# Layer 1's SwiGLU FFN: gate and up by seven block products instead of eight, with the second products set between the next chunk's first ones

## The chip, the cores and the metric

One core of a Trainium2 chip runs the program. The metric is the device time of one execution in microseconds; the kernel before took 1693.99 us in the median of three runs (1692.38 to 1694.93). Matrix products run on TensorE, the rest on VectorE, ScalarE and GpSimd; DMAs are issued from SyncE's queue (SP).

## What is computed

A two-layer backbone over 512 latent tokens and 256 context tokens of width 1024. Each layer mixes tokens in four head groups and then applies a modulated SwiGLU FFN with 2816 hidden columns, 22 tiles of 128. The change is in the FFN of the latent tokens in the second layer (layer 1), the last work before the output:

```python
def swiglu(h, w_in_, w_out_):
    gate, up = jnp.split(h @ w_in_, 2, axis=-1)
    return (jax.nn.silu(gate) * up) @ w_out_
...
    x = x + g_a * rms_norm(mix_x @ w_out, norm_g[1])
    x = x + g_f * rms_norm(swiglu(modulate(rms_norm(x, norm_g[2]), sh_f, sc_f), w_ffn_in, w_ffn_out), norm_g[3])
```

All of it is float32.

## The kernel before

**Numbers as hi and lo.** Matrices are kept as a rounded hi and the rest lo (`split`, L363: hi on ScalarE, L366; lo on VectorE or GpSimd, L367). A product of 128 rows is three matmuls (`mac3`): hi by hi (L425), hi by lo (L426 or L427) and lo by hi. In them the weights of a hidden tile are the stationary operand and the tokens the moving one, 512 columns, or 256 where a product is made in halves of the tokens.

**Weights.** `weights` (L372) loads a raw unit (512 KB for eight 128 by 128 tiles) into one of four buffers of the pool `wr` and splits it in two pieces of 512 columns into the pools `wh` (five buffers) and `wl` (four). `lo_pool` alternates the engine of the lo. `prefetch` loads units early into slots of their own (`wt`).

**The FFN** (`ffn`, L1462; called from `layer_end`). The 22 hidden tiles come in chunks, `fcx`: (0, 8), (8, 15), (15, 22). For each hidden tile j there are two units, gate and up, each a product over eight k tiles: 48 matmuls into two PSUM tiles. `ffn_gate` (L1452) makes tanh on ScalarE (L1456), two VectorE instructions on PSUM and SBUF (L1457, L1458) and a split into `g` (L369, L370). In layer 1 the first three tiles (`first1`) are made in halves of the tokens, since the second half of the activations `hf` is ready later. After a chunk's hidden tiles come its eight second products (one for each 128 columns of the output), 3 matmuls for each hidden tile of the chunk, added into `y` by `evac_y` (L1404 on ScalarE for the first chunk, L1406 on VectorE for the others). The last chunk's last five are made in halves again, then `ends` applies the norm and the residual (L545, L546) and stores x. The stream x stays in SBUF all the time.

**Order.** A scheduler of the framework sets the order of each engine's instructions from the dependences and the order of the program; buffers of pools are given out in turn, so a load waits until the last reader of the buffer's former content is done.

Of the kernel before, what the change touches and what calls it, by code (L numbers as in the profile page):

```python
# [21 lines left out]
P = 128  # L22
D = 1024
KT = D // P
# [11 lines left out]
# how the work is cut and which engine takes what  # L36
# [24 lines left out]
 'preu1': 4,  # L61
# [46 lines left out]
 'por': '1023'}  # L108
# [20 lines left out]
class Half:  # L129
    """Half a slot; the slot is given back with the second of them."""  # L130
# [10 lines left out]
class Arena:  # L141
    """Equal slots of SBUF, taken and given back in program order."""
# [35 lines left out]
class HL:  # L178
    """A float32 matrix [K, N] as hi + lo, in tiles of 128 rows."""
# [21 lines left out]
class F32T:  # L201
    """A float32 matrix [K, N] in tiles of 128 rows."""
# [15 lines left out]

class Stream:
# [3 lines left out]
class Build:  # L223
    def __init__(self, tc, es, I, out, dbg=None):
# [7 lines left out]
        self.wl = pool("wl", bufs=T["wl"])  # L232
        self.ap = pool("arena", bufs=1)
# [23 lines left out]
    def scale(self, c, out, in_, col):  # L257
        """out = in_ * col on the engine that c names."""
# [75 lines left out]
    def load_params(self, l, p=None):  # L334
        """The layer's small parameters; those of the norms first."""
# [26 lines left out]
    def split(self, hi, lo, src, scale=None, eng=None):  # L362
        """hi = round(src * scale), lo = src * scale - hi; both exact in float32r."""  # L363
# [8 lines left out]
    def weights(self, src, shape, hold=False):  # L372
        """A unit of weights from DRAM: shape[0] matrices of shape[1] columns as (hi, lo). With hold in slots, until freed."""
# [29 lines left out]
    def prefetch(self, units, hold=0):  # L403
        """Loads the units that the next calls of weights ask for, the first ones held in slots."""
# [5 lines left out]
    def tick(self):  # L410
        """Emits work of the background at its rate."""
# [11 lines left out]
    def mac3(self, out, lh, ll, rh, rl, first, last):  # L423
        nc = self.nc
        nc.tensor.matmul(out, lh, rh, start=first, stop=False)  # L425
        nc.tensor.matmul(out, lh, rl, start=False, stop=False)  # L426
        nc.tensor.matmul(out, ll, rh, start=False, stop=last)  # L427

    def dense(self, out, w, a, t0, n, w0=0, nk=KT, late=False, ks=None):
        """out[128, n] = w^T a over nk tiles of rows, tokens t0..t0+n; w from its tile w0 on. With late a's lo comes last."""  # L430
        nc = self.nc
        ks = ks or range(nk)
        for i in ks:
            f, z = i == ks[0], i == ks[-1]
            ah, al = a.h[i][:, t0:t0 + n], a.l[i][:, t0:t0 + n]
# [15 lines left out]
    def rsqrt(self, y, v, tag):  # L451
        """y = 1/sqrt(v) on small tiles of float32."""
# [3 lines left out]
    def rms(self, tiles, t0, n):  # L456
        """PSUM tile [128, n]: rstd of the tokens t0..t0+n in every partition; tiles: 8 of [128, .]."""
# [5 lines left out]
    def square(self, sq, k, x, n, t0=0, full=None, evac=False):  # L463
        """Squares of x, tile k of 8, for columns t0..t0+n: two sums, of the even and of the odd tiles, but for the last two."""
# [23 lines left out]
    def rms_end(self, parts, n, norm=False):  # L488
        """The same from the squares, in parts to be summed."""
# [28 lines left out]
    def modnorm(self, st, h, A, B, t0, n):  # L518
        """h (hi, lo) = rms_norm(x) * A + B for the tokens t0..t0+n of the stream."""
# [15 lines left out]
    def residual(self, st, y, G, t0, n, sq):  # L535
        """x += G * rms_norm(y) for the tokens t0..t0+n."""
# [1324 lines left out]
```

## Time and profile before

| | |
|---|---|
| runs (3) | 1694.93, 1693.99, 1692.38 us; median 1693.99 |
| span of the profiled execution | 1692.6 us (the page has no other time of it) |
| TensorE busy | 1624.3 us, 96%, 9935 matmuls |
| VectorE, ScalarE, GpSimd busy | 944.4, 740.5, 607.2 us |
| read from and written to HBM | 209.14 MB, 4.19 MB |

A busy share is an average over stages; what a stage is limited by is read from the stretch itself, and there from who waits for whom. Recorded matmuls overlap: what one costs is seen from one start to the next. The stretch of the change begins near 1337 us and goes to the end.

### The profile page before, as it was taken

How to read it: one execution, taken by the hardware profiler on the slowest of the kernel's cores; microseconds unless marked ns; L12 is line 12 of the kernel's file. 1: busy time of each engine (PE TensorE's matmuls, PEld its weight loads, DVE VectorE, ACT ScalarE, POOL GpSimd, SP SyncE). 2: the span in 40 equal slices, each digit the busy share in tenths (PEclk: the TensorE clock that was granted, in tenths of full speed). 3: DMA queues.
4: the chain of work that ended last, by engine and by line, in shares of the span. 5: the costliest groups of instructions: out<-in, count | busy, mean ns of one | idle time of the engine just before them, and what ended most of it. 6: DMA issues, size and time to landing. Idle time of an engine off the chain costs nothing.

```text
span 1692.6 us, 27131 instructions
## 1 busy us (share of the span) xinstructions
PE 1624.3 (96%) x9935; PEld 1381.3 (82%) x9935; DVE 944.4 (56%) x2172; ACT 740.5 (44%) x1658; POOL 607.2 (36%) x691
## 2 busy tenths in 40 slices
PE   6899999999999999999999998999798999999997
PEld 2876778787989998888888888999578988888887
DVE  4876675858685569542443466758765531232344
ACT  3654456654445655333332334465565433332331
POOL 2421333664466565322222225332425322222233
PEclk9999999999999998999999998999799999999998
DMA  9554564254466423334334452122042122323221
GB/s 315 178 181 154 190 222 125 98 176 129 148 230 184 148 74 116 112 138 149 138 127 150 137 201 95 59 73 70 2 132 81 38 93 94 98 82 107 92 95 51
DMA packets 81045, 215.10 MB, mean 127 GB/s; under 512 B 10512, under 2 KB 18576, under 8 KB 80912
## 3 DMA queue, kind: packets, MB, share of 16 engines
q1 hardware_dynamic: 80912, 213.37, 38.3%
q8 instruction: 78, 1.28, 0.3%
q14 instruction: 55, 0.45, 0.1%
HBM read 209.14 MB, written 4.19 MB: 126 GB/s over the span
## 4 chain that ended last, share of the span: by engine, by line
PE 83%; DVE 8%; DMA 3%; issue 2%; ACT 2%; POOL 1%; SPq 0%; DVEq 0%; POOLq 0%; ACTq 0%
PE mm L425 22%; PE mm L427 22%; PE mm L426 22%; PE ms L584 2%; PE mx L1097 2%; PE mm L437 1%; PE mx L1091 1%; PE mm L438 1%; DMA wm_m<-in_wmod_dram 1%; PE mx L1349 1%; PE mm L449 1%; PE mm L443 1%; PE mm L442 1%; PE mm L444 1%; DVE wl L367 1%
## 5 line engine op out<-in xcount | busy, mean ns | idle before, releaser
L366 ACT ACTIVATE wh<-wr 128x512 fp32r<-128x512 f32 (+3 forms) x526 | 318.9, 616 | 581.5 <-PE mm L426 478.9
L367 POOL TENSOR_TENSOR wl<-wr,wh 128x512 fp32r<-128x512 f32 (+2 forms) x248 | 322.8, 1304 | 666.1 <-PE mm L427 517.8
L367 DVE TENSOR_TENSOR wl<-wr,wh 128x512 fp32r<-128x512 f32 (+3 forms) x278 | 206.7, 747 | 180.5 <-PE mm L427 131.5
L425 PE MATMUL mm<-hfh_m,wh 128*128 128x512 f32 (+1 forms) x656 | 253.7, 387 | 0.0
L426 PE MATMUL mm<-hfl_m,wh 128*128 128x512 f32 (+1 forms) x656 | 253.5, 386 | 0.0
L427 PE MATMUL mm<-hfh_m,wl 128*128 128x512 f32 (+1 forms) x656 | 253.4, 386 | 0.0
L425 PEld LDWEIGHTS mm<-hfh_m,wh 128*128 128x128 f32 x656 | 123.7, 188 | 26.5
L427 PEld LDWEIGHTS mm<-hfh_m,wl 128*128 128x128 f32 x656 | 123.5, 188 | 26.5
L426 PEld LDWEIGHTS mm<-hfl_m,wh 128*128 128x128 f32 x656 | 123.5, 188 | 26.5
L425 PE MATMUL mm<-gh_m,wh 128*128 128x512 f32 x275 | 108.3, 394 | 0.0
L426 PE MATMUL mm<-gl_m,wh 128*128 128x512 f32 x275 | 108.1, 394 | 0.0
L427 PE MATMUL mm<-gh_m,wl 128*128 128x512 f32 x275 | 108.0, 393 | 0.0
L1458 DVE TENSOR_TENSOR ft_m<-mm,ft_m 128x512 f32<-128x512 f32 (+1 forms) x50 | 31.3, 626 | 133.2 <-PE mm L427 131.7
L426 PE MATMUL mm<-hfl_c,wh 128*128 128x256 f32 x352 | 100.3, 285 | 1.0 <-POOL hfl_c L532 1.0
L425 PE MATMUL mm<-hfh_c,wh 128*128 128x256 f32 x352 | 99.9, 285 | 0.0
L427 PE MATMUL mm<-hfh_c,wl 128*128 128x256 f32 x352 | 99.2, 283 | 0.0
L627 DVE SCALAR_TENSOR_TENSOR macc_m<-wr,cs,macc_m 128x512 f32<-128x512 f32 x56 | 44.1, 787 | 65.8 <-DMA wr<-in_wmod_dram 64.8
L425 PEld LDWEIGHTS mm<-hfh_c,wh 128*128 128x128 f32 x352 | 66.2, 188 | 4.0 <-issue 3.4
L426 PEld LDWEIGHTS mm<-hfl_c,wh 128*128 128x128 f32 x352 | 66.3, 188 | 2.3 <-POOL hfl_c L532 1.2
L427 PEld LDWEIGHTS mm<-hfh_c,wl 128*128 128x128 f32 x352 | 66.1, 188 | 1.3 <-issue 1.0
L1406 DVE TENSOR_TENSOR y_m<-mm,y_m 128x256 f32<-128x256 f32 (+1 forms) x43 | 23.6, 551 | 68.2 <-PE mm L427 68.2
L427 PEld LDWEIGHTS mm<-gh_m,wl 128*128 128x128 f32 x275 | 51.7, 188 | 12.0
(597 smaller groups left out, 4165.5 us busy)
## 6 DMA issues: line engine op xcount, KB each, us to landing
wr<-in_wfi_dram SPq DMA_DIRECT2D x132, 512.0 KB, 3.6
wr<-in_wmod_dram SPq DMA_DIRECT2D x80, 512.0 KB, 3.6
wr<-in_wT_dram SPq DMA_DIRECT2D x42, 512.0 KB, 3.8
wr<-in_wfo_dram SPq DMA_DIRECT2D x32, 512.0 KB, 3.5
wr<-in_wfo_dram SPq DMA_DIRECT2D x32, 448.0 KB, 3.3
wr<-in_wo_dram SPq DMA_DIRECT2D x24, 512.0 KB, 3.6
wm_m<-in_wmod_dram SPq DMA_DIRECT2D x32, 256.0 KB, 5.3
wr<-in_wRB_dram SPq DMA_DIRECT2D x12, 384.0 KB, 3.3
```

Source lines behind the costliest of these rows:

```text
L366: nc.scalar.activation(hi, src, AF.Copy)
L367: (eng or nc.vector).tensor_tensor(out=lo, in0=src, in1=hi.bitcast(F32), op=ALU.subtract)
L425: nc.tensor.matmul(out, lh, rh, start=first, stop=False)
L426: nc.tensor.matmul(out, lh, rl, start=False, stop=False)
L427: nc.tensor.matmul(out, ll, rh, start=False, stop=last)
L437: nc.tensor.matmul(out, w.h[w0 + i], ah, start=f, stop=False)
L438: nc.tensor.matmul(out, w.l[w0 + i], ah, start=False, stop=False)
L584: nc.tensor.matmul(ps[o:o + 32, :], self.cs[:, k, :], ws[i], start=True, stop=True, tile_position=(0, o))
L627: nc.vector.scalar_tensor_tensor(out=t, in0=w, scalar=self.cs[:, k, s:s + 1], in1=t, op0=ALU.mult, op1=ALU.add)
L1097: nc.tensor.matmul(po[kv * 64:kv * 64 + 64, 0:256], stream.av.t[b][:, kv * 64:kv * 64 + 64], pts[kv].t[:, i * 256:(i + 1) * 256], start=i0 ...
L1406: nc.vector.tensor_tensor(out=yt, in0=ps, in1=yt, op=ALU.add)
L1458: nc.vector.tensor_tensor(out=a, in0=pu, in1=a, op=ALU.mult)
```

## The change

In layer 1 alone (`'strassen': (1,)`), for hidden tiles 4 to 21, gate and up together are taken as one product of a 2 by 2 block matrix. The blocks of the weights are (gate or up) by (first or second half of the 1024 rows), those of the activations (halves of the rows) by (halves of the 512 tokens). Eight block products become seven, by Winograd's form of Strassen's method: four sums of weight blocks for each hidden tile (`strassen_pair`, L1547 in the changed kernel), four sums of activation blocks once (`strassen_rhs`, L1513), and the results put together in PSUM: products 0, 2, 4 and 6 go on in one PSUM tile `z`, 3 and 5 in `w`, 1 in `y`, and what stands in `z` after products 0, 2 and 4 is read before the next of them is added. Each product has 4 k tiles by 3 matmuls of 256 columns. Raw weights and weight sums are split per product: seven hi's on ScalarE, four lo's on GpSimd and three on VectorE (`slo`). Hidden tile 3 is still made in eight block products, in two halves of 256 columns.

The chunks become (0, 4), (4, 8), (8, 12), (12, 15), (15, 22), and the eight second products of a chunk are emitted between the products of the next chunk's tiles, in PSUM tiles of the ring `mx`. To make room, x is stored to DRAM before the sums and loaded again after the last pair. `wr` and `wl` have five buffers instead of four, a new pool `ws` six, and one hidden tile less is prefetched (`preu1` 3 for 4). Lines of the changed kernel are 39 or more higher: `split` has its lo in L406, `mac3` L464 to L466.

```diff
- 'wr': 4,
+ 'wr': 5,
...
- 'wl': 4,
+ 'wl': 5,
...
- 'preu1': 4,
+ 'preu1': 3,
...
+ 'strassen': (1,),
+ 'fcs': ((0, 4), (4, 8), (8, 12), (12, 15), (15, 22)),
+ 'sad': 'PPVV',
+ 'slo': 'PVVPPVP',
+ 'sre': 'VPVP',
+ 'srt': 'VPVP',
+ 'srl': 'VPVP',
+ 'sup': 'V',
+ 'sgl': 'V',
+ 'ws': 6}
...
+    def strassen_rhs(self, h):
...
+        (b11, b12), (b21, b22) = h.blocks
+        out = [HL(self.ar, f"st{i}", KT // 2, h.half) for i in range(4)]
...
+        for i in range(KT // 4):
...
+            tt(e[0], x11, x12, x11)
+            tt(e[1], x12, x22, x12)
+            tt(e[2], x22, x22, x11)
+            tt(e[3], x21, x21, x22)
+            for m, (t, v) in enumerate(((out[1], x22), (out[0], x11), (out[2], x12), (out[3], x21))):
+                self.split(t.slots[i][0].t[:, 0:n], t.slots[i][1].t[:, 0:n], v, eng=self.e(T["srl"][m]))
...
+        return out, [b11, b21, out[1], out[0], out[2], b22, out[3]]
...
+    def strassen_pair(self, l, j, h, rhs, g, jj):
...
+        tt(ad[0], s[0], a21, a22, ALU.add)
+        tt(ad[1], s[2], a11, a21, ALU.subtract)
+        tt(ad[2], s[1], s[0], a11, ALU.subtract)
+        tt(ad[3], s[3], a12, s[1], ALU.subtract)
+        lhs = [a11, a12, s[1], s[0], s[2], s[3], a22]
...
+        for i in range(7):
...
+            self.split(hi, lo, lhs[i], eng=self.e(T["slo"][i]))
...
+            ps, first = [(z, True), (y, True), (z, False), (w, True), (z, False), (w, False), (z, False)][i]
+            for k in range(KT // 2):
+                c = slice(k * P, k * P + P)
+                self.mac3(ps[:, 0:n], hi[:, c], lo[:, c], rhs[i].h[k], rhs[i].l[k], first and k == 0, k == KT // 2 - 1, not first)
+            if i == 0:
+                nc.scalar.activation(p1, z[:, 0:n], AF.Copy, scale=0.5)
+            elif i == 1:
+                nc.vector.scalar_tensor_tensor(out=c1t[:, 0:n], in0=y[:, 0:n], scalar=0.5, in1=p1, op0=ALU.mult, op1=ALU.add)
+            elif i == 2:
+                nc.scalar.activation(q, z[:, 0:n], AF.Copy, scale=0.5)
+            elif i == 3:
+                nc.scalar.activation(p5t, w[:, 0:n], AF.Copy)
+            elif i == 4:
+                nc.vector.tensor_tensor(out=c2t, in0=z[:, 0:n], in1=p5t, op=ALU.add)
+                p5.free()
+            elif i == 5:
+                nc.vector.scalar_tensor_tensor(out=c1t[:, n:2 * n], in0=w[:, 0:n], scalar=0.5, in1=q, op0=ALU.mult, op1=ALU.add)
...
+        nc.scalar.activation(a, c1t, AF.Tanh)
+        nc.vector.scalar_tensor_tensor(out=a, in0=a, scalar=1.0, in1=c1t, op0=ALU.add, op1=ALU.mult)
+        nc.vector.tensor_tensor(out=a[:, 0:n], in0=z[:, 0:n], in1=a[:, 0:n], op=ALU.mult)
+        tt(T["sup"], a[:, n:2 * n], a[:, n:2 * n], c2t, ALU.mult)
+        self.split(g.h[jj], g.l[jj], a, eng=self.e(T["sgl"]))
...
+    def ffn_seven(self, l, st, h, G, chunks, first, hold, last, hold2, then, between, after):
...
+        for k in range(KT):
+            self.nc.sync.dma_start(out=st.src[:, k, :], in_=st.x[k])
+        self.drop_x(st)
+        sums, rhs = self.strassen_rhs(h)
...
+        for ci, (k0, k1) in enumerate(rest):
+            gn = HL(self.ar, "g", k1 - k0, n)
+            outs = self.ffn_tiles(l, y, g, j0, j1, KT, n, sq, ci == 0, False, self.mx)
+            total, done = 7 * (k1 - k0), 0
+            for i, _ in enumerate(self.strassen_tiles(l, k0, k1, h, rhs, gn)):
+                while done * total < (i + 1) * KT:
+                    next(outs)
+                    done += 1
...
+        self.load_x(st, st.src)
```

TensorE's order before, in layer 1's FFN, at the step from one unit of weights to the next (`hfh`, `hfl` are the activations' hi and lo, `wh` and `wl` those of the weights):

```order
8016 L425 MATMUL mm_16204<-hfh_m_14620,wh_16199 128x512
8017 L426 MATMUL mm_16204<-hfl_m_14621,wh_16199 128x512
8018 L427 MATMUL mm_16204<-hfh_m_14620,wl_16200 128x512
8019 L425 MATMUL mm_16279<-hfh_m_14606,wh_16261 128x512
8020 L426 MATMUL mm_16279<-hfl_m_14607,wh_16261 128x512
8021 L427 MATMUL mm_16279<-hfh_m_14606,wl_16262 128x512
```

Each PSUM tile `mm` takes one unit's 24 matmuls of 512 columns, one behind the other. TensorE's order in the changed kernel, within hidden tile 4 (`hf00` to `hf11` are the blocks of the activations, `st0` to `st3` their sums, `mx` a second product, `gh` the hidden layer):

```order
7437 L464 MATMUL mm_15446<-hf10h_m_14619,wh_15442 128x256
7438 L465 MATMUL mm_15446<-hf10l_m_14620,wh_15442 128x256
7439 L464 MATMUL mx_15428<-gh_m_14849,wh_15424 128x512
7440 L466 MATMUL mm_15446<-hf10h_m_14619,wl_15443 128x256
7441 L464 MATMUL mm_15481<-st0h_m_15317,wh_15477 128x256
7442 L465 MATMUL mx_15428<-gl_m_14850,wh_15424 128x512
7443 L466 MATMUL mx_15428<-gh_m_14849,wl_15425 128x512
7444 L464 MATMUL mm_15401<-st1h_m_15321,wh_15460 128x256
```

Product 1 (`hf10`), a second product, product 3 (`st0`) and product 2 (`st1`) follow each other within a few matmuls; the matmuls of pairs have 256 columns.

GpSimd's order before, hidden tiles in the FFN of layer 1, two rows for each tile:

```order
600 L367 TENSOR_TENSOR wl_16262<-wr_16259,wh_16261 128x512
601 L367 TENSOR_TENSOR wl_16272<-wr_16269,wh_16271 128x512
602 L367 TENSOR_TENSOR wl_16338<-wr_16335,wh_16337 128x512
603 L367 TENSOR_TENSOR wl_16348<-wr_16345,wh_16347 128x512
604 L367 TENSOR_TENSOR wl_16414<-wr_16411,wh_16413 128x512
```

and in the changed kernel, in the last chunk, from one tile's sums to the next's:

```order
673 L1547 TENSOR_TENSOR ws_17798<-wr_17796 128x512
674 L1547 TENSOR_TENSOR ws_17800<-wr_17794,wr_17796 128x512
675 L406 TENSOR_TENSOR wl_17704<-ws_17639,wh_17703 128x512
676 L406 TENSOR_TENSOR wl_17722<-ws_17641,wh_17721 128x512
677 L406 TENSOR_TENSOR wl_17758<-wr_17755,wh_17757 128x384
678 L406 TENSOR_TENSOR wl_17773<-wr_17637,wh_17772 128x512
679 L406 TENSOR_TENSOR wl_17811<-wr_17794,wh_17810 128x512
680 L1547 TENSOR_TENSOR ws_17957<-wr_17955 128x512
681 L1547 TENSOR_TENSOR ws_17959<-wr_17953,wr_17955 128x512
```

There are two sums and four lo's for each tile, and now and then the lo of a second product's weights (`128x384`). Rows 680 and 681 read the raw unit `wr_17955`. SP's order in the changed kernel at that place:

```order
493 L1543 DMA wr_17637<-in_wfi_dram 128x1024
494 L419 DMA wr_17755<-in_wfo_dram 128x384
495 L1543 DMA wr_17794<-in_wfi_dram 128x1024
496 L1543 DMA wr_17796<-in_wfi_dram 128x1024
497 L419 DMA wr_17897<-in_wfo_dram 128x384
498 L1543 DMA wr_17953<-in_wfi_dram 128x1024
499 L1543 DMA wr_17955<-in_wfi_dram 128x1024
```

The two raw units of a tile are issued together (`wr_17953`, `wr_17955`); one of them takes the buffer of `wr_17637`, which GpSimd reads last in its row 678.

## Rows read from the trace of the kernel before

One execution, one core. Times are microseconds unless a row says ns; L and a number is a line of the kernel; PE is TensorE, PEld its weight loads, DVE VectorE, ACT ScalarE, POOL GpSimd; an x before a number is a count.

**Rows 1.** the page's busy time, share of the span and instructions of each engine.

```profile
PE 1624.3 (96%) x9935; PEld 1381.3 (82%) x9935; DVE 944.4 (56%) x2172; ACT 740.5 (44%) x1658; POOL 607.2 (36%) x691
```

**Rows 2.** the page's chain that ended last, share by engine and by line.

```profile
PE 83%; DVE 8%; DMA 3%; issue 2%; ACT 2%; POOL 1%; SPq 0%; DVEq 0%; POOLq 0%; ACTq 0%
PE mm L425 22%; PE mm L427 22%; PE mm L426 22%; PE ms L584 2%; PE mx L1097 2%; PE mm L437 1%; PE mx L1091 1%; PE mm L438 1%; DMA wm_m<-in_wmod_dram 1%; PE mx L1349 1%; PE mm L449 1%; PE mm L443 1%; PE mm L442 1%; PE mm L444 1%; DVE wl L367 1%
```

**Rows 3.** busy time of each engine by stretch; columns in the first line.

```profile
core 0: us, PE busy (x) PEld busy (x) DVE busy (x) ACT busy (x) POOL busy (x), PEclk, DMA share, GB/s
400.00:560.00 160.00, 156.85 (x1268) 145.69 (x1267) 105.36 (x263) 72.94 (x159) 90.99 (x97) 0.98 0.54 173
1290.00:1340.00 50.00, 45.07 (x356) 44.10 (x355) 36.23 (x70) 25.38 (x62) 25.42 (x29) 0.93 0.20 64
1340.00:1640.00 300.00, 300.00 (x1313) 244.05 (x1312) 82.70 (x126) 97.10 (x165) 74.30 (x58) 1.00 0.30 96
```

**Rows 4.** who waited for what, 1290 to 1692 us: total us, times, longest.

```profile
POOL wl L367 <- PE mm L427: 223.8, 56, 7.1
ACT wh L366 <- PE mm L426: 194.5, 108, 3.9
DVE wl L367 <- PE mm L427: 101.1, 27, 5.2
```

**Rows 5.** groups by form, 1290 to 1692.6 us: busy us, mean ns | idle before.

```profile
L427 PE MATMUL mm<-hfh_m,wl 128*128 128x512 f32 x304 | 119.9, 394 | 0.0
L367 POOL TENSOR_TENSOR wl<-wr,wh 128x512 fp32r<-128x512 f32 x58 | 75.5, 1301 | 230.4 <-PE mm L427 223.8 <-ACT wh L366 6.6
L366 ACT ACTIVATE wh<-wr 128x512 fp32r<-128x512 f32 x107 | 67.5, 632 | 181.8 <-PE mm L426 178.8 <-DMA wr<-in_wfi_dram 3.0
L367 DVE TENSOR_TENSOR wl<-wr,wh 128x512 fp32r<-128x512 f32 x49 | 34.8, 709 | 101.9 <-PE mm L427 97.6 <-issue 4.3
L370 DVE SCALAR_TENSOR_TENSOR gl_m<-ft_m,gh_m 128x512 fp32r<-128x512 f32 x19 | 14.2, 750 | 1.9 <-ACT gh_m L369 0.2
L1458 DVE TENSOR_TENSOR ft_m<-mm,ft_m 128x512 f32<-128x512 f32 x19 | 13.1, 691 | 70.3 <-PE mm L427 70.3
L1457 DVE SCALAR_TENSOR_TENSOR ft_m<-ft_m,mm 128x512 f32<-128x512 f32 x19 | 13.0, 686 | 4.0 <-ACT ft_m L1456 4.0
L1456 ACT ACTIVATE ft_m<-mm 128x512 f32<-128x512 f32 x19 | 11.0, 580 | 0.0
L1406 DVE TENSOR_TENSOR y_m<-mm,y_m 128x256 f32<-128x256 f32 x10 | 4.2, 420 | 10.3 <-PE mm L427 10.3
```

**Rows 6.** TensorE's timeline, second products, 1399.62 to 1409.81: start us, us.

```profile
1399.62 0.39 PE L425 MATMUL mm<-gh_m,wh 128*128 128x512 f32 x1
1409.81 0.39 PE L427 MATMUL mm<-gh_m,wl 128*128 128x512 f32 x1
```

**Rows 7.** TensorE's timeline, last matmuls in token halves, from 1337.71.

```profile
1337.71 0.28 PE L425 MATMUL mm<-hfh_m,wh 128*128 128x256 f32 x1
1341.14 0.28 PE L427 MATMUL mm<-hfh_m,wl 128*128 128x256 f32 x1
```

**Rows 8.** busy time by stretch, columns as in rows 3: last products in halves.

```profile
1652.00:1664.00 12.00, 12.00 (x102) 11.87 (x101) 3.93 (x8) 2.31 (x5) 1.47 (x2) 1.00 0.00 1
```

**Rows 9.** VectorE's timeline around 119.4 us.

```profile
119.41 1.42 DVE L367 TENSOR_TENSOR wl<-wr,wh 128x512 fp32r<-128x512 f32 x1 [1.27 <-ACT wh L366]
```

**Rows 10.** GpSimd's timeline around 119 us.

```profile
118.99 1.30 POOL L367 TENSOR_TENSOR wl<-wr,wh 128x512 fp32r<-128x512 f32 x1 [14.52 <-ACT wh L366]
```

**Rows 11.** GpSimd's timeline, the last lo's of hf.

```profile
1330.63 1.70 POOL L532 TENSOR_TENSOR hfl_m<-mn_t,hfh_m 128x256 fp32r<-128x256 f32 x2 [0.87 <-ACT mn_t L531]
```

**Rows 12.** TensorE's timeline, its first 512-column matmul of the stretch.

```profile
1343.36 0.39 PE L425 MATMUL mm<-hfh_m,wh 128*128 128x512 f32 x1
```

**Rows 13.** DMA issues, 1340 to 1640 us: KB each, median us to landing.

```profile
wr<-in_wfi_dram SPq DMA_DIRECT2D x34, 512.0 KB, 3.5
wr<-in_wfo_dram SPq DMA_DIRECT2D x15, 448.0 KB, 3.2
```

More of the change, by code (lines that the diff above doesn't have):

```diff
@@ L216, in free, with __init__, __getitem__ @@
             s.free()
+class Pair:
+    def __init__(self, a, b, n):
+        self.a, self.b, self.n = a, b, n
+    def __getitem__(self, at):
+        rows, c = at
+        if c.stop <= self.n:
+            return self.a[rows, c]
+        return self.b[rows, c.start - self.n:c.stop - self.n]
+class Quarters:
+    def __init__(self, ar, name, nk, n):
+        self.half = n // 2
+        blocks = [[HL(ar, f"{name}{i}{j}", nk // 2, n // 2) for j in range(2)] for i in range(2)]
+        self.blocks = blocks
+        self.h = [Pair(blocks[k * 2 // nk][0].h[k % (nk // 2)], blocks[k * 2 // nk][1].h[k % (nk // 2)], n // 2) for k in range(nk)]
+        self.l = [Pair(blocks[k * 2 // nk][0].l[k % (nk // 2)], blocks[k * 2 // nk][1].l[k % (nk // 2)], n // 2) for k in range(nk)]
+    def free(self):
+        for b in sum(self.blocks, []):
+            b.free()
 class Stream:
@@ L434, in dense @@
             f, z = i == ks[0], i == ks[-1]
+            if isinstance(a, Quarters) and n > a.half:
+                for q in range(2):
+                    c = slice(q * a.half, q * a.half + a.half)
+                    self.mac3(out[:, c], w.h[w0 + i], w.l[w0 + i], a.h[i][:, c], a.l[i][:, c], f and q == 0, z and q == 1, True)
+                continue
             ah, al = a.h[i][:, t0:t0 + n], a.l[i][:, t0:t0 + n]
@@ new lines, in strassen_tiles, with ffn_tiles, body @@
+    def strassen_tiles(self, l, j0, j1, h, rhs, g):
+        for j in range(j0, j1):
+            yield from self.strassen_pair(l, j, h, rhs, g, j - j0)
+    def ffn_tiles(self, l, y, g, j0, j1, whole, n, sq, first, end, ring):
+        for m in range(whole):
+            w = self.weights(*self.ffo(l, m, j0, j1))
+            ps = ring()
+            self.dense(ps[:, 0:n], w, g, 0, n, nk=j1 - j0)
+            self.evac_y(y, m, ps[:, 0:n], 0, n, sq, first, end)
+            yield
+    def ffn_seven(self, l, st, h, G, chunks, first, hold, last, hold2, then, between, after):
+        n = st.n
+        sq = []
+        win = lambda j, u: (self.I["wfi"][l, j, u], (KT, P))
+        (j0, j1), rest = chunks[0], chunks[1:]
+        g = HL(self.ar, "g", j1 - j0, n)
+        pair = []
+        def body(i, ps, t0):
+            pair.append(ps)
+            if len(pair) == 2:
+                self.ffn_gate(g, i // 2, *pair, t0, n // 2)
+                pair.clear()
+        self.halved([win(j, u) for j in range(first) for u in range(2)], h, n, body, hold, late=T["latef"])
+        if between:
+            between()
+        for j in range(first, j1):
+            wg, wu = self.weights(*win(j, 0)), self.weights(*win(j, 1))
+            pg, pu = self.mm(), self.mm()
+            self.dense(pg, wg, h, 0, n)
+            self.dense(pu, wu, h, 0, n)
+            self.ffn_gate(g, j, pg, pu, 0, n)
+        st.src = self.dr.tile([P, KT, n], F32, tag=f"xs{l}", name=f"xs{l}")
+        for k in range(KT):
+            self.nc.sync.dma_start(out=st.src[:, k, :], in_=st.x[k])
+        self.drop_x(st)
+        sums, rhs = self.strassen_rhs(h)
+        y = F32T(self.ar, "y", KT, n)
+        for ci, (k0, k1) in enumerate(rest):
[6 more added lines that the diff above has]
+                    done += 1
+            self.all(outs)
+            g.free()
+            g, j0, j1 = gn, k0, k1
+        h.free()
+        for t in sums:
+            t.free()
+        self.load_x(st, st.src)
+        nk = j1 - j0
+        self.all(self.ffn_tiles(l, y, g, j0, j1, last, n, sq, False, True, self.mm))
+        body = lambda i, ps, t0: self.evac_y(y, last + i, ps, t0, n // 2, sq, False, True, n)
+        mark = self.halved([self.ffo(l, m, j0, j1) for m in range(last, KT)], g, n, body, hold2, nk=nk)
+        self.ends(st, y, G, sq, mark, then, g.free, after)
+        y.free()
```

66 lines of the change are left out of this document (59 added, 7 removed).

## Prediction

> **What bounds the kernel now.** The profiled execution spans 1692.6 us; the page gives no other time of its own for it, and its span is 1.4 below the median of the three runs, 1693.99, and inside their spread (1692.38 to 1694.93). I make the sum against the median. Faster or slower means by over 0.2% (3.4 us, about what a measurement of this kernel can tell from no change): below 1690.6, above 1697.4.
>
> I read the shares first: TensorE is busy 96% of the span, VectorE 56%, ScalarE 44%, GpSimd 36% [rows 1]. The chain that ended last goes the same way: 83% of it is TensorE, the three matmul lines of `mac3` alone 66% [rows 2]. Then the stretch that the change rewrites, layer 1's FFN from 1340 to 1640 us: TensorE 300.00 of 300 at full granted clock, VectorE 82.70, ScalarE 97.10, GpSimd 74.30, DMA share 0.30 [rows 3]. Last, who waits for whom there: the engines that prepare weights wait for TensorE to give buffers back, GpSimd 223.8 us, ScalarE 194.5, VectorE 101.1 [rows 4]. So here a matmul taken away is time won, as long as preparing weights stays hidden.
>
> **What a matmul costs.** Recorded durations overlap (394 ns, [rows 5]), so I take the distance from start to start. With 512 columns, 44 steps from 1399.62 to 1409.81: 0.2316 us [rows 6]. With 256 columns and the same operands, 29 steps from 1337.71 to 1341.14: 0.1183 [rows 7]; later, 102 in 12.00 us: 0.1176 [rows 8]. I take 0.118.
>
> **Matmuls removed.** A hidden tile was 2 x 8 x 3 = 48 matmuls of 512 columns: 11.12 us. By seven products it is 7 x 4 x 3 = 84 of 256: 9.91. That saves 1.21, and on 18 tiles (j = 4 to 21) 21.7 us. Tile j = 3 becomes 96 of 256 columns, 11.33: 0.2 lost. The second products stay 528 matmuls of 512 columns, only set between others. Net **-21.5** (-21.0 with 0.1183, -22.0 with 0.1176): with TensorE as dense as now, 1672.5.
>
> **Work added, per hidden tile.** GpSimd had two lo's at most (1.301 us each, [rows 5]); now two weight sums and four lo's. No row shows a sum of weights; it has the lo's shape and one f32 output, so I take 1.30 too: 6 x 1.30 = 7.8. VectorE gets two sums and three lo's (0.709 each by the same rows), plus the gate's pieces (0.69 to 0.75 for 512 columns, about 0.42 for 256). ScalarE gets seven hi's (0.632), three copies of 256 columns (below the 580 ns that a tanh of 512 takes), a tanh and a hi: under 7.4. Each alone lies under a tile's 9.91 plus the second products set beside it: in chunks of four tiles 2 x 12 x 0.2316 = 5.56, together 15.47; in the chunk of three 17.3; in the last chunk, seven tiles to eight products of nine matmuls, 2.38, together **12.29**.
>
> But GpSimd and VectorE don't add up freely. At 119.41 a VectorE lo of 512 columns took 1.42 us [rows 9], where its like takes 0.709; it began inside a GpSimd lo that ran from 118.99 to 120.29 [rows 10], and ended 0.54 after it. So a VectorE instruction with both inputs in SBUF waits GpSimd's out and then needs 0.54. Reads of PSUM show no such stretch (L1458: 691 ns, [rows 5]). The Trainium skill states it as a rule (SBUF — State Buffer, "Who interferes with whom"): GpSimd and VectorE's second port pair share one exclusive lock. By it, and by the row, their occupancies add; without it this term would be nothing.
>
> Added up for the last chunk: GpSimd 7.8 plus four lo's of second products in seven tiles (three quarters of 1.30 each) 0.56; VectorE 7 x 0.54 = 3.78, half an instruction for 256 columns 0.27, its own lo's of second products 0.23. That is 12.64 against 12.29 of TensorE: the pair becomes the bound by 0.35 at the least, if they never stand idle. They do: GpSimd's first sum needs the tile's second raw load, whose slot comes free with GpSimd's own lo two rows before it. I take 0.9 us per tile, **+6.3** on seven (0: all side by side; 18 and more: rivals B and C). In chunks of four the sum is 9.1 + 4.6 = 13.7 of 15.47 and in that of three no nearer: 0 (up to 0.4 per tile, 3).
>
> **The sums of activations at the start.** Two rounds of six GpSimd, six VectorE and four ScalarE instructions. They can start when hf's second half is whole, 1332.3 [rows 11], and product 2 of tile 4 needs the first ones. TensorE's first 512-column matmul is at 1343.36 [rows 12]; from there tile 3 (11.33), two products (2.83) and one second product (2.78) bring product 2 to 1360.3. GpSimd has 12 of these plus five of its usual by then, 17 x 1.30 = 22.1, to 1354.4; with 12 x 0.54 of VectorE shut in, 1360.9, and later sums and lo's behind it. I take **+2.5** (0 to 6: all of VectorE's and two more lo's behind).
>
> **x in DRAM.** Eight stores and eight loads of 256 KB on SP's queue. A load of 512 KB lands 3.5 us after its issue and one of 448 KB after 3.2 [rows 13], and the stretch's DMA share is 0.30. The stores are issued while tile 3 runs; the first second-product load behind them has tile 3 and two products, 14 us, of cover. The loads mix with the five last second-product loads, some behind slots that the last products give back; some 45 matmuls of 512 columns, 10.4 us, run before those weights are due, against 3.2 and a preparation of 0.63 + 1.30. I take **+1** (0 to 4). One more slot for wr and wl and one prefetched unit less move rows on every engine through the whole program: no row prices that; 0, between -3 and +3.
>
> **Sum**: 1694.0 - 21.5 + 6.3 + 2.5 + 1 = **1682.3**.
>
> **Rivals.**
> **A, all preparation hidden.** For it: from 400 to 560 us GpSimd is busy 90.99 and VectorE 105.36 of 160 and TensorE still 156.85 [rows 3]. Against: there many VectorE instructions read PSUM or are short. Stalls of 0 to 3: 1672.5 to 1677.
> **B, GpSimd's wait for the load isn't filled in the last chunk.** Its first sum waits for a load issued when its lo two rows before ends: 3.5 less the one lo between, 1.30, leaves 2.2 standing per tile. If VectorE's work doesn't fall into it, a tile takes 12.64 + 2.2 = 14.84, 2.55 over TensorE, 17.9 on seven: 1672.5 + 17.9 + 3.5 = 1693.9, no change.
> **C, the other side.** The same place, but the lo between doesn't fill either, because it waits for a buffer of its own: GpSimd stands the whole 3.5, a tile takes 16.14, 3.85 over, 27.0 on seven: 1672.5 + 27.0 + 3.5 = 1703.0, slower. It decides at about 2.7 us of standing per tile. Against: wr, wl and the sums' pool have five to six buffers, so loads run up to two tiles ahead.
> **D, 256 columns cost more than half in this mix.** The stretch around 1290 to 1340, mostly 256-column work, gives 45.07 us busy for 356 matmuls, 0.127 [rows 3]: a tile saves 0.45 and tile 3 loses 1.1, so -7.0, with the stalls 1696.8. Against: [rows 7, 8] are this very form, at 0.118. The Trainium skill (TensorE: Matmul & The Clock Gate, "Why this matters for your kernels") asks for all dimensions of 512 or more to reach 85% of peak; a half at 85% would be an estimated 0.136 and the kernel 1701. The trace disagrees: 2% is lost, not 15%.
> That the products aren't made as described is excluded by the order of the changed kernel, which has the 18 x 84.
>
> **How the numbers follow.** Forecast 0.46 (1677 to 1690), A 0.28, B 0.13 (0.05 of it below 1690.6), C 0.09, D 0.04 (0.01 of it slower). Faster 0.46 + 0.28 + 0.05 = 0.79; the same 0.08 + 0.03 = 0.11; slower 0.10. The range 1670 to 1695 holds the forecast, A with the -3 of the moved rows, and most of B; it leaves out C and D.
>
> **What would show it.** TensorE's 256-column matmuls with hf and st still 0.118 apart; in the four-tile chunks TensorE without gaps; in the last chunk gaps of about 1 us per tile before products, ended by GpSimd or VectorE `wl`, and VectorE lo's well above 0.709 on average; a gap of 2 to 3 us near 1360. Gaps in every chunk, or gaps ended by ScalarE's copies of PSUM, would make it wrong, as would a stretch without any (A). GpSimd waiting for in_wfi loads over 2 us per tile means B or C.

## The result, and the profile after

The changed kernel takes 1707.35 us in the median of four runs (1702.13 to 1709.61) against 1693.57 for the kernel before on the same chip: a ratio of 1.0072, 95% interval 1.0052 to 1.0093 (the two medians alone give 1.0081). It is slower by 0.7 to 0.8%; the forecast was 1682.3, faster, with a range of 1670 to 1695. The profiled execution took 1706.92 us and spans 1705.1.

The page of the changed kernel, first the busy time by engine (as [rows 1]):

```profile
PE 1606.2 (94%) x10631; PEld 1403.3 (82%) x10631; DVE 1109.2 (65%) x2326; ACT 790.4 (46%) x1774; POOL 745.9 (44%) x775
```

TensorE is busy 18 us less than before, as meant, but for 94% of a longer span; VectorE is busy 165 us more, GpSimd 139. By stretch, the one of the FFN (columns as in [rows 3]):

```profile
1340.00:1640.00 300.00, 284.26 (x1997) 264.54 (x1996) 226.45 (x267) 142.06 (x267) 197.47 (x133) 0.98 0.30 94
```

Where TensorE had 300.00 of 300 us and a clock of 1.00, it now has 284.26 and 0.98.

Two landmarks cut the span, both read from TensorE's timeline: the end of the last product of the first three hidden tiles (in token halves), and the end of the last second product.

| kernel | up to the landmark | FFN from there | rest | span |
|---|---|---|---|---|
| before | 1337.9 | 340.8 | 13.9 | 1692.6 |
| changed | 1345.4 | 345.8 | 13.9 | 1705.1 |

So 7.5 us were lost ahead of everything that the change is about, and the FFN, which should have become 21.5 us shorter, became 5.0 longer: 26.5 us of new loss. I added up each step from one matmul to the next over 0.2316 and 0.118 us: between the landmarks there are gaps of 7.2 us from 1354 to 1375, 1.5 in the four- and three-tile chunks and 12.4 from 1552 to 1660 (the last chunk), and 5.3 us of steps that are a little longer (2.2 at the start, 0.2 in between, 2.9 in the last chunk), most of them matmuls at nearly twice their distance. The sum is 26.4. The rest, 1172 matmuls from 1380 to 1552, stands 0.2 us off the two distances besides those gaps.

The first gap, in TensorE's timeline of the changed kernel (start, duration, and in brackets the idle time before and what ended it):

```profile
1374.44 0.80 PE L465 MATMUL mx<-gl_m,wh 128*128 128x512 f32 x1 [4.76 <-DVE gl_m L409]
...
1375.67 0.42 PE L465 MATMUL mm<-st1l_m,wh 128*128 128x256 f32 x1
...
1379.82 0.28 PE L465 MATMUL mm<-st0l_m,wh 128*128 128x256 f32 x1
```

TensorE waited 4.76 us for `gl_m`, the lo of tile 3's hidden layer, and then matmuls of 256 columns took 0.42 us apiece in the records until 1379.5, where those at full clock take 0.28. The granted clock of these stretches, and VectorE and GpSimd just before the gap:

```profile
1350.00:1360.00 10.00, 9.79 (x84) 9.58 (x83) 10.00 (x9) 3.36 (x7) 9.37 (x7) 1.00 0.17 37
1374.40:1380.00 5.60, 5.56 (x25) 5.38 (x26) 3.20 (x4) 2.02 (x4) 2.32 (x2) 0.53 0.18 47
1583.50:1590.00 6.50, 6.48 (x38) 6.34 (x39) 5.16 (x7) 2.86 (x6) 3.36 (x3) 0.74 0.26 78
```

0.53 is the lower of the two levels (1.2 of 2.4 GHz) for nearly all of 5.6 us; what TensorE did before it fell was to stand for 4.8 us. Behind a gap of 2.2 us that began at 1581, a part of the third row is at the lower level too. From 1350 to 1360 VectorE has no free moment (10.00 of 10), GpSimd 0.63.

What VectorE and GpSimd did before `gl_m` came, first VectorE, then GpSimd:

```profile
1350.80 1.77 DVE L406 TENSOR_TENSOR st2l_m<-sx_m,st2h_m 128x512 fp32r<-128x512 f32 x1
1352.50 1.80 DVE L406 TENSOR_TENSOR wl<-wr,wh 128x512 fp32r<-128x512 f32 x1
1354.22 1.77 DVE L406 TENSOR_TENSOR st1l_m<-sx_m,st1h_m 128x512 fp32r<-128x512 f32 x1
...
1370.98 1.74 DVE L1547 TENSOR_TENSOR ws<-ws,wr 128x512 f32<-128x512 f32 x1 [2.75 <-POOL ws L1547]
1372.64 1.75 DVE L409 SCALAR_TENSOR_TENSOR gl_m<-ft_m,gh_m 128x512 fp32r<-128x512 f32 x1
```

```profile
1350.55 1.48 POOL L1513 TENSOR_TENSOR sx_m<-sx_m,sx_m 128x512 f32<-128x512 f32 x1
1351.99 1.76 POOL L406 TENSOR_TENSOR st0l_m<-sx_m,st0h_m 128x512 fp32r<-128x512 f32 x1
1353.68 1.75 POOL L1513 TENSOR_TENSOR sx_m<-sx_m,sx_m 128x512 f32<-128x512 f32 x1
...
1369.68 1.26 POOL L1547 TENSOR_TENSOR ws<-wr 128x512 f32<-128x512 f32 x1 [2.60 <-PE mm L464]
1370.90 1.27 POOL L1547 TENSOR_TENSOR ws<-wr,wr 128x512 f32<-128x512 f32 x1
```

Two things are to be seen. From 1350.5 on the two engines go in step, one instruction each in 1.7 us, where one alone takes 0.69 on VectorE and 1.30 on GpSimd. It is the same in the whole stretch from 1345 to 1650: 81 VectorE instructions of 512 columns with both inputs in SBUF began during one of GpSimd's, and 80 of them ended 0.54 to 0.56 us after it (1.76 us each in the median); the 53 that met none took 0.69. So the mechanism that the prediction read from one pair of rows holds throughout. And at 1370.98 VectorE's first sum of the next tile's weights stands in its queue ahead of `gl_m`: it had waited 2.75 us for GpSimd's sum, which had itself waited for TensorE; `gl_m` came behind it, though TensorE stood for it.

The groups of the FFN's stretch, 1345 to 1650 us (busy time, mean ns of one, idle time before and its releasers, as [rows 5]):

```profile
L406 POOL TENSOR_TENSOR wl<-wr,wh 128x512 fp32r<-128x512 f32 x51 | 76.1, 1501 | 33.4 <-ACT wh L405 33.0
L406 POOL TENSOR_TENSOR wl<-ws,wh 128x512 fp32r<-128x512 f32 x36 | 59.7, 1673 | 17.7 <-ACT wh L405 17.6
...
L406 DVE TENSOR_TENSOR wl<-wr,wh 128x512 fp32r<-128x512 f32 x32 | 35.2, 1099 | 4.6 <-ACT wh L405 3.4
L406 DVE TENSOR_TENSOR wl<-ws,wh 128x512 fp32r<-128x512 f32 x36 | 34.4, 956 | 5.1 <-ACT wh L405 3.8
L1547 DVE TENSOR_TENSOR ws<-ws,wr 128x512 f32<-128x512 f32 x17 | 29.7, 1744 | 18.9 <-POOL ws L1547 18.9
...
L406 DVE TENSOR_TENSOR gl_m<-fe_m,gh_m 128x512 fp32r<-128x512 f32 x17 | 24.7, 1453 | 1.6 <-ACT gh_m L405 1.5
...
L1547 POOL TENSOR_TENSOR ws<-wr 128x512 f32<-128x512 f32 x17 | 23.2, 1365 | 50.0 <-DMA wr<-in_wfi_dram 47.4 <-PE mm L464 2.6
...
L1450 DVE TENSOR_TENSOR y_m<-mx,y_m 128x512 f32<-128x512 f32 x24 | 16.4, 684 | 11.6 <-PE mx L466 11.6
```

GpSimd's lo's, 1301 ns before, take 1501 and 1673; VectorE's, 709 before, 1099 and 956, and its first sum 1744. What reads PSUM keeps its time (L1450, 684). GpSimd's first sum waited 47.4 us in all for its raw load, in the list of waits of the same stretch (total, times, longest), and 15.1 of it in the last chunk, 1552 to 1645, where VectorE in turn waited for GpSimd's sums:

```profile
POOL ws L1547 <- DMA wr<-in_wfi_dram: 47.4, 15, 5.6
```

```profile
POOL ws L1547 <- DMA wr<-in_wfi_dram: 15.1, 5, 5.6
...
DVE ws L1547 <- POOL ws L1547: 8.8, 5, 2.4
```

The gaps of the last chunk, TensorE's timeline:

```profile
1560.26 0.50 PE L466 MATMUL mx<-gh_m,wl 128*128 128x512 f32 x1 [1.05 <-DVE wl L406]
...
1569.62 0.39 PE L466 MATMUL mm<-st0h_m,wl 128*128 128x256 f32 x1 [1.59 <-POOL wl L406]
...
1583.52 0.39 PE L464 MATMUL mm<-st3h_m,wh 128*128 128x256 f32 x1 [2.01 <-DVE fd_m L1581]
```

They end with whatever was last in either queue: a lo of VectorE, a lo of GpSimd, VectorE's reading of a product (`fd_m`, L1581).

### The profile page after: what moved, and what is told of

It is laid out like the page before. It is cut to its first block, busy times and chain, and to the rows that moved or that the text cites. A ratio compares the mean times of both kernels' runs of the same rounds, so it can differ in the third digit from the quotient of the medians.

```text
span 1705.1 us, 28934 instructions
## 1 busy us (share of the span) xinstructions
PE 1606.2 (94%) x10631; PEld 1403.3 (82%) x10631; DVE 1109.2 (65%) x2326; ACT 790.4 (46%) x1774; POOL 745.9 (44%) x775
## 5 line engine op out<-in xcount | busy, mean ns | idle before, releaser
L406 POOL TENSOR_TENSOR wl<-wr,wh 128x512 fp32r<-128x512 f32 (+2 forms) x248 | 335.1, 1357 | 498.3 <-ACT wh L405 464.0
L405 ACT ACTIVATE wh<-wr 128x512 fp32r<-128x512 f32 (+2 forms) x508 | 308.9, 617 | 465.1 <-PE mm L465 328.4
L406 DVE TENSOR_TENSOR wl<-wr,wh 128x512 fp32r<-128x512 f32 (+3 forms) x260 | 214.8, 829 | 120.0 <-ACT wh L405 117.4
L464 PE MATMUL mm<-hfh_m,wh 128*128 128x512 f32 (+1 forms) x320 | 124.8, 390 | 0.0
L466 PE MATMUL mm<-hfh_m,wl 128*128 128x512 f32 (+1 forms) x320 | 124.4, 389 | 0.0
L465 PE MATMUL mm<-hfl_m,wh 128*128 128x512 f32 (+1 forms) x320 | 124.1, 388 | 0.0
L466 PE MATMUL mm<-hfh_c,wl 128*128 128x256 f32 x352 | 100.1, 285 | 0.0
L464 PE MATMUL mm<-hfh_c,wh 128*128 128x256 f32 x352 | 99.7, 284 | 0.0
L466 PEld LDWEIGHTS mm<-hfh_m,wl 128*128 128x128 f32 x320 | 60.1, 188 | 13.5
L465 PEld LDWEIGHTS mm<-hfl_m,wh 128*128 128x128 f32 x320 | 60.2, 188 | 13.0
L464 PEld LDWEIGHTS mm<-hfh_m,wh 128*128 128x128 f32 x320 | 60.2, 188 | 12.9
L464 PEld LDWEIGHTS mm<-hfh_c,wh 128*128 128x128 f32 x352 | 66.2, 188 | 5.3 <-issue 2.3
L466 PEld LDWEIGHTS mm<-hfh_c,wl 128*128 128x128 f32 x352 | 66.4, 189 | 1.5 <-issue 0.6
L406 POOL TENSOR_TENSOR wl<-ws,wh 128x512 fp32r<-128x512 f32 x36 | 59.7, 1673 | 17.7 <-ACT wh L405 17.6
L464 PE MATMUL mm<-gh_m,wh 128*128 128x512 f32 x155 | 61.3, 398 | 2.1 <-ACT wh L405 1.5
L466 PE MATMUL mm<-gh_m,wl 128*128 128x512 f32 x155 | 60.9, 394 | 0.0
L465 PE MATMUL mx<-gl_m,wh 128*128 128x512 f32 x120 | 48.0, 400 | 6.2 <-DVE gl_m L409 4.8
```

The source lines that it names most:

```text
L405: nc.scalar.activation(hi, src, AF.Copy)
L406: (eng or nc.vector).tensor_tensor(out=lo, in0=src, in1=hi.bitcast(F32), op=ALU.subtract)
L464: nc.tensor.matmul(out, lh, rh, start=first, stop=False, skip_group_check=more)
L465: nc.tensor.matmul(out, lh, rl, start=False, stop=False, skip_group_check=more)
L466: nc.tensor.matmul(out, ll, rh, start=False, stop=last, skip_group_check=more)
```

## The experiments

All ratios are to the kernel before on the same chip, whose median was between 1693.6 and 1695.3 us. "FFN" is the length between the two landmarks of the table above in the profiled execution.

**The FFN of before in the changed buffers.** `'strassen': ()`: TensorE's order up to the FFN is the changed kernel's, but for 60 of 8318 matmuls just ahead of the landmark.

```diff
- 'strassen': (1,),
+ 'strassen': (),
```

> The changed kernel with the seven products switched off: layer 1's FFN is again the one of before, in the changed kernel's buffers (wr and wl five, one unit less prefetched); up to the FFN, TensorE's order is the changed kernel's. In the trace of the changed kernel the FFN's last product in token halves already ends 7.6 us later than before. Theory 1, the new order of the work ahead of the FFN costs that much: 1699 to 1702. Rival, it is scatter between executions or comes from the FFN's own buffers: 1692 to 1696.

1700.30 us, ratio 1.0031 (1.0018 to 1.0043); FFN 340.7, as before. The new order ahead of the FFN costs 5.2 us by the medians. Two of TensorE's waits from 1030 to 1260 us (total, times, longest) have grown, the kernel before and then this one:

```profile
PE ms L504 <- DVE sq_t L479: 4.6, 1, 4.6
PE mx L1381 <- DVE ht_m L750: 3.5, 2, 2.6
```

```profile
PE mx L1425 <- DVE ht_m L794: 7.8, 3, 3.4
PE ms L548 <- DVE sq_t L523: 7.2, 1, 7.2
```

The same two waits, for VectorE's `ht_m` in the mixing of the tokens and for the squares of the norm, are longer by 4.3 and 2.6 us. The place of the landmark differs between executions too: 1337.9 to 1340.2 in the four profiles with four and four buffers, 1341.9 to 1348.2 in the seven with five and five, and the changed kernel's own order gave 1341.9 in one run and 1345.4 in two. So the 7.5 us of the table hold for one execution, and the 5.2 of the medians are the better figure.

**Four buffers for wr and wl.**

```diff
- 'wr': 5,
+ 'wr': 4,
...
- 'wl': 5,
+ 'wl': 4,
```

> The changed kernel with wr and wl of four buffers as before; TensorE's order ahead of the FFN is then that of before, and the FFN has the seven products. Theory 1: the 7 us ahead of the FFN come back, 1699 to 1702, and less if the FFN does with four. Rival, the fifth buffers carry the FFN's loads and the gain ahead is lost again there: 1706 or more, with GpSimd's wait for in_wfi loads over the 47 us of the changed kernel.

1694.52 us, 0.9994 (0.9984 to 1.0004): no difference from before. It is 4.5 us under the lower end of what was expected: the landmark comes at 1340.2, and the FFN, at 340.3, is not longer but shorter than with five. That the FFN needs the fifth buffers is refuted; with four the change as such is worth nothing, and costs nothing.

**More cover in the last chunk.**

```diff
- 'fcs': ((0, 4), (4, 8), (8, 12), (12, 15), (15, 22)),
+ 'fcs': ((0, 4), (4, 8), (8, 12), (12, 17), (17, 22)),
```

> The changed kernel with chunks (0,4), (4,8), (8,12), (12,17), (17,22): every tile then has at least 4.4 us of second products beside it, where the tiles of the last chunk had 2.4. Theory 2, the stalls of the last chunk (11 us and a spell of the lower clock) come from the lack of cover for GpSimd and VectorE: 1694 to 1698. Rival, they come from the raw loads, whose number is the same: 1704 or more.

1700.44 us, 1.0035 (1.0022 to 1.0049). FFN 339.3, 6.6 less than the change; the rest behind it is 16.0 us, 2.1 longer. The result lies between the two expectations. From 1552 on 1.1 us of gaps are left up to 1655 and 1.8 there; 5 us near 1366 stay, and the chunks before have 5.5. Thin cover was part of the cause, not all of it.

**Everything on VectorE.**

```diff
- 'sad': 'PPVV',
- 'slo': 'PVVPPVP',
- 'sre': 'VPVP',
- 'srt': 'VPVP',
- 'srl': 'VPVP',
+ 'sad': 'VVVV',
+ 'slo': 'VVVVVVV',
+ 'sre': 'VVVV',
+ 'srt': 'VVVV',
+ 'srl': 'VVVV',
```

> The changed kernel with all sums and all lo's of the seven products on VectorE and none on GpSimd. Theory 3, GpSimd and VectorE shut each other out (GpSimd's lo of a sum took 1.67 us here for 1.30, VectorE's sums 1.74 for 0.7): VectorE alone does 11 x 0.69 per tile, and the stalls at the start and in the last chunk shrink, 1690 to 1698. Rival, the amount of work and not the lock: VectorE then has some 12.2 us per tile for 12.3 of TensorE in the last chunk, and the stalls stay or grow, 1707 or more.

1684.26 us, 0.9937 (0.9922 to 0.9951), 6 under the expected range and 23 off the changed kernel, for moving work off an engine that was busy 66% of this stretch onto one that was busy 75%. FFN 321.9, with gaps of 1.3 us, all in the last chunk. Its groups:

```profile
L406 DVE TENSOR_TENSOR wl<-ws,wh 128x512 fp32r<-128x512 f32 x72 | 50.9, 709 | 4.4 <-ACT wh L405 2.8
...
L406 DVE TENSOR_TENSOR wl<-wr,wh 128x512 fp32r<-128x512 f32 x68 | 46.2, 685 | 6.6 <-ACT wh L405 5.4
...
L1547 DVE TENSOR_TENSOR ws<-wr 128x512 f32<-128x512 f32 x17 | 12.8, 755 | 15.2 <-DMA wr<-in_wfi_dram 15.2
...
L1547 DVE TENSOR_TENSOR ws<-ws,wr 128x512 f32<-128x512 f32 x17 | 11.6, 683 | 0.0
```

140 lo's in 97.1 us where 68 took 69.6; the sum at 1744 ns takes 683. By stretch (the start, the chunks between, the last chunk; columns as in [rows 3]):

```profile
1345.00:1380.00 35.00, 35.00 (x276) 33.95 (x275) 29.79 (x51) 19.20 (x37) 7.08 (x3) 1.00 0.25 73
1380.00:1550.00 170.00, 170.00 (x1179) 158.06 (x1178) 128.80 (x224) 85.77 (x159) 13.96 (x11) 1.00 0.32 100
1550.00:1640.00 90.00, 89.33 (x640) 83.28 (x639) 73.87 (x129) 47.76 (x95) 12.39 (x9) 1.00 0.39 125
```

VectorE does 232 us in these 295; in the changed kernel it was busy 221, GpSimd 193. It is only 11 us busier than when it shared the work.

**Only the sums of the activations on VectorE.**

```diff
+ 'sre': 'VVVV',
+ 'srt': 'VVVV',
+ 'srl': 'VVVV',
```

> The changed kernel with only the sums of the activations on VectorE; the hidden tiles' sums and lo's stay as the change has them, and TensorE's order is the changed kernel's. Theory: the gap near 1370 us (4.9 us and a spell of the lower clock) goes, 8 to 10 us: 1697 to 1700; the stalls of the last chunk stay. Rival, the gap is the lateness of tile 3's gate behind VectorE's queue, which gets longer: 1707 or more.

1696.68 us, 1.0008 (0.9994 to 1.0021). The gap near 1370 is gone, FFN 336.3, 9.6 less; the gaps of the last chunk stand as they were (1.2, 1.7, 2.2, 1.9 us). The rival, by which more work in VectorE's queue makes `gl_m` later still, falls: VectorE had more to do and `gl_m` came in time, though a sum of weights still stood ahead of it in the queue.

**Only the tiles' sums and lo's on VectorE.**

```diff
+ 'sad': 'VVVV',
+ 'slo': 'VVVVVVV',
```

> The counterpart: only the hidden tiles' sums and lo's on VectorE, the sums of the activations shared with GpSimd as the change has them. Theory: the last chunk's stalls (11 us and 1.7 of the lower clock) go, the gap near 1370 stays: 1693 to 1697, and with the run before this one the two gains make up the 23 us of all on VectorE. Rival, the gap at the start alone carries it: 1704 or more.

1687.68 us, 0.9954 (0.9940 to 0.9967), 5.3 under the expected range. FFN 325.3, 20.5 less; a gap of 3.1 us at 1367 stays, in the last chunk 0.9 of gaps are left. The two shares, 9.6 and 20.5, come to more than the 24.0 of both: each of the two runs took away a part of the loss near 1370 (9.0 and 5.3 us).

**The lock by itself.** All on VectorE again, and six additions for each tile on GpSimd which read a hi and write a tile that nobody reads.

```diff
...
+            for _ in range((2, 0, 0, 2, 1, 0, 1)[i]):
+                nc.gpsimd.tensor_tensor(out=self.dum, in0=hi.bitcast(F32), in1=hi.bitcast(F32), op=ALU.add)
...
```

> All on VectorE as in the run at 1684.3 us, plus six additions of 128x512 on GpSimd for each hidden tile, which read a hi of the weights and write a tile that nobody reads: the same work for VectorE, and GpSimd busy as in the changed kernel. Theory, the lock: VectorE's lo's rise from 0.70 us to 1.0 or more and TensorE's gaps in the last chunk come back, 1690 to 1702. Rival, amount alone (VectorE has the same amount, nobody waits for GpSimd): 1683 to 1686 and lo's of 0.70.

1713.87 us, 1.0112 (1.0080 to 1.0144), 30 us more than without the additions and 12 over the upper end. FFN 353.7, with gaps of 27.8 us.

```profile
L1565 POOL TENSOR_TENSOR dum_m<-wh 128x512 f32<-128x512 f32 x108 | 141.4, 1309 | 122.2 <-ACT wh L405 113.4 <-DVE fe_m L1592 3.3 <-DVE ws L1547 1.2
L406 DVE TENSOR_TENSOR wl<-wr,wh 128x512 fp32r<-128x512 f32 x68 | 72.1, 1074 | 0.1
L406 DVE TENSOR_TENSOR wl<-ws,wh 128x512 fp32r<-128x512 f32 x72 | 68.0, 947 | 0.8 <-ACT wh L405 0.6
...
L406 POOL TENSOR_TENSOR wl<-wr,wh 128x512 fp32r<-128x512 f32 x13 | 23.4, 1800 | 9.1 <-ACT wh L405 9.1
...
L1547 DVE TENSOR_TENSOR ws<-wr 128x512 f32<-128x512 f32 x17 | 15.1, 886 | 12.4 <-DMA wr<-in_wfi_dram 12.3
```

VectorE has the same instructions as at 1684.3 and its lo's take 1074 and 947 ns for 685 and 709. VectorE's wait for raw loads has not grown with the gaps: 12.3 us, where it was 15.2 without the additions. What TensorE waits for in this stretch:

```profile
PE mm L466 <- DVE wl L406: 10.6, 10, 3.3
PE mm L464 <- ACT wh L405: 3.2, 2, 2.7
```

The largest part of its waits ends with VectorE, none with GpSimd. (ScalarE waited 5.0 us for the additions to give back a hi, so a little of the 30 us may be that.)

**All on VectorE, four buffers.**

```diff
+ 'wr': 4,
...
+ 'wl': 4,
...
+ 'sad': 'VVVV',
+ 'slo': 'VVVVVVV',
+ 'sre': 'VVVV',
+ 'srt': 'VVVV',
+ 'srl': 'VVVV',
```

> All sums and lo's of the seven products on VectorE, and wr and wl of four buffers: the order of the work ahead of the FFN is that of before. Theory: the two gains add, 1684.3 less the 5 us that the buffers cost ahead of the FFN: 1676 to 1680. Rival, the FFN needs the fifth buffers when VectorE alone makes the sums: 1684 or more, with PE gaps ended by VectorE's wl behind a wait for in_wfi loads.

1676.98 us, 0.9886 (0.9860 to 0.9913), within the expectation: faster than both kernels. Landmark at 1339.6, FFN 323.1.

**Which of the buffers.** All on VectorE and one of the two pools at four, first `wl`, then `wr`.

```diff
+ 'wl': 4,
```

> All sums and lo's of the seven products on VectorE, wr five and wl four buffers (1684.3 us with five and five, 1677.0 with four and four). If the raw buffers alone move the order ahead of the FFN: 1682 to 1686. If they do nothing there: 1675 to 1679.

1685.67 us, 0.9949 (0.9929 to 0.9968).

```diff
+ 'wr': 4,
```

> The counterpart, wr four and wl five. If the lo's buffers alone move the order: 1682 to 1686. If they do nothing there: 1675 to 1679.

1677.98 us, 0.9902 (0.9878 to 0.9926). By the medians it is the fifth raw buffer that costs: 8.7 us over four and four, against 1.0 for the lo's buffer, where the intervals of the two ratios overlap. Both move the order: up to the landmark TensorE's differs from that of the kernel before in 2153 of 8318 places with the raw buffer and in 2840 with the lo's. What the order costs where isn't settled by the two waits of the first experiment, here with the raw buffer and then with the lo's:

```profile
PE ms L548 <- DVE sq_t L523: 6.2, 2, 6.0
PE mx L1425 <- DVE ht_m L794: 3.5, 2, 2.6
```

```profile
PE mx L1425 <- DVE ht_m L794: 7.0, 3, 2.9
PE ms L548 <- DVE sq_t L523: 4.9, 2, 4.6
```

`ht_m` is waited for longer with the lo's buffer, which costs next to nothing by the medians, and not with the raw one.

**More cover besides.** The kernel at 1676.98 with the chunks of the third experiment.

```diff
+ 'fcs': ((0, 4), (4, 8), (8, 12), (12, 17), (17, 22)),
```

> All on VectorE, four and four buffers, and the chunks (0,4), (4,8), (8,12), (12,17), (17,22). Three gaps of together 3.1 us are left in the last chunk at 1677.0. Theory, thin cover there: they go, but the last second products get shorter and their loads closer together: 1673 to 1677. Rival, the end is then late for its weights: 1678 or more.

1675.87 us, 0.9887 (0.9866 to 0.9907): the interval is that of the run at 1676.98, so no gain is shown. The gaps of the last chunk are gone (FFN 320.3), but the waits behind the last product got longer (2.2 and 2.0 us for the squares' sums, 1.6 and 0.5 before).

## Why the prediction was wrong

**Right: the matmuls.** 48 of 0.2316 us against 84 of 0.118 held. With the preparation out of the way the FFN is 321.9 and 323.1 us long where 340.8 - 21.5 = 319.3 was forecast for dense TensorE. That excludes rival D. The row of the Trainium skill that was set beside D (TensorE: Matmul & The Clock Gate, "Why this matters for your kernels") asks for a total of 20 GFLOP besides the dimensions of 512; it speaks of whole products, not of single matmuls in a dense stream, so the 15% were no fair reading of it, and no run here tests it.

**Wrong: "I take 0.9 us per tile" for the last chunk, +6.3.** It was 12.4 us of gaps and 2.9 of longer steps, 2.2 us per tile. The occupancies were added up well: in step the two engines take 1.7 us for a pair of instructions where I had 1.30 + 0.54. The failing part is what followed: a sum that leaves no slack was given a small price for standing. The pair did stand: from 1552 to 1645 GpSimd waited 15.1 us for raw loads, 2.2 per tile, which is what rival B put there, and VectorE's work didn't fill it. That each late load left one engine idle and then put both to work at once, where they are slowest, is how I read the timelines; no run shows it apart.

**Wrong: "+2.5 (0 to 6)" for the start.** 7.2 us of gaps and 2.2 of slower matmuls. I counted the sums of activations against product 2 and not what stands with them in VectorE's queue: the gate's lo of tile 3, which the first second products need. Moving those sums alone gave 9.6 us back.

**Wrong: no term for the clock.** After gaps of 4.9 and 2.2 us TensorE ran at the lower level: 5.6 us at a mean of 0.53 and 6.5 at 0.74, which is 5.6 x 0.47 + 6.5 x 0.26, about 4 us. They are among the 2.2 and 2.9 us of longer steps above (and a little of the gaps), and don't come on top.

**Wrong: "0, between -3 and +3" for the moved rows.** 5.2 us by the medians, 8.7 for the fifth raw buffer with all on VectorE; no row priced them, and the bounds that I set were too narrow.

**x in DRAM, +1**, isn't settled. The rest behind the last product is 13.9 us as before. The gap of 0.8 us at 1660 is ended by ScalarE's hi of the last tile's hidden layer, not by anything of x. A gap of 1.6 us at 1645 is ended by the hi of a second product's weights, after ScalarE had waited 3.1 us for a load on the queue that x's loads share; that x delayed it isn't shown.

**A slower result** came as a sum of these. Rival B's place and wait were right for the last chunk (17.9 us forecast, 15.3 measured), and its 1693.9, less those 2.6 us, with 6.8 more at the start, 7.5 ahead of the FFN and 1.7 in the chunks between comes to about 1707. That rival C's 1703 lies near the result is luck: it has 27.0 us for the last chunk. That the tiles with 5.56 us of cover stall little (1.5 us of gaps in eleven tiles) was right.

Shown by runs: that GpSimd working beside VectorE lengthens VectorE's instructions and costs this kernel some 30 us (the idle additions), that moving the work off GpSimd takes 23 us away, the shares of the start and of the last chunk in that, and the price of the raw buffer by the medians. Not separated: how much of the last chunk's loss is the lock itself, how much GpSimd's standing for loads and how much VectorE's waiting for GpSimd's sums; all on VectorE takes away all three, and the additions bring back the first without the others. Only argued: why the FFN with five buffers is 5.5 us longer than with four in the change as it was made (345.8 and 340.3), when with all on VectorE it is not (321.9 and 323.1).

## What to carry to other kernels

Before sharing vector work between VectorE and GpSimd, add the two up as one engine wherever VectorE's instructions have both inputs in SBUF; if an instruction costs 0.7 us on VectorE and 1.3 on GpSimd, sharing makes it 1.7 for two where VectorE alone needs 1.4. A preparation whose occupancies add up to TensorE's time per tile (12.64 against 12.29 us by the forecast's sum here) is not hidden: any standing of its engines, here 2.2 us per tile for loads, turns into gaps, and a gap can cost again at the lower clock. And a buffer more in a pool that the whole program uses moved the order of thousands of matmuls in stages that the change doesn't touch: measure it apart from the change that it comes with.

## What was not expected of the hardware

GpSimd pays too: its lo's took 1501 and 1673 ns on average for 1301, so the engine that is supposed to help becomes slower by 15 to 29%. The Trainium skill's rule (SBUF — State Buffer, "Who interferes with whom") has the order of issue decide which of the two waits. That agrees with the trace of the changed kernel in both directions: a VectorE instruction that began second ended 0.55 us after GpSimd's, and GpSimd's of 512 columns that began during one of VectorE's ended 1.15 us after it in the median, for 1.29 alone. The additions that nobody needed paid as well: the 101 of 108 that began during a VectorE instruction with both inputs in SBUF took 1.37 us in the median, the other seven 1.04. VectorE's lo's rose in that run by a third (947 for 709 ns) to over a half (1074 for 685).

And one gap of 2.2 us was followed by a spell at the lower clock, where others of 2.1 and 1.8 us in the same chunk were not:

```profile
1613.00:1620.00 7.00, 6.59 (x47) 6.09 (x47) 6.29 (x10) 3.78 (x8) 3.87 (x3) 1.00 0.31 88
1569.60:1573.00 3.40, 3.18 (x23) 2.96 (x24) 3.30 (x6) 1.42 (x3) 1.96 (x2) 1.00 0.01 2
```
